# Seven products with eight sums: products that add up in shared PSUM banks, in the output projections and the feed-forward part of a hybrid block

## The chip, the cores and the metric

One Trainium2 chip, one of its cores. The metric is the device time of one execution in microseconds. PE is the matrix engine, DVE, ACT and POOL are the vector, scalar and GpSimd engines, SP issues most of the DMAs.

## The reference

A transformer block on one sequence of 1024 tokens of width 1024, in float32:

```python
h = rms_norm(x, norm1_gain)
hq, hf, hi, hg, sq, sk, sv, ga, gb = split_cols(h @ w_in, IN_SPLITS)
y_hg = (rms_norm(hgrn2_mixer(hq, hf, hi, lb)) * sigmoid(hg)) @ w_hg_out     # 1024 x 1024
y_sb = stick_breaking(rms_norm(sq), rms_norm(sk), sv) @ w_sb_out            # 1024 x 1024
x = x + (sigmoid(ga) * y_hg + sigmoid(gb) * y_sb) @ w_o                     # 1024 x 1024
gate, up = split_cols(rms_norm(x, norm2_gain) @ w_ffn_in, (2816, 2816))
x = x + (silu(gate) * up) @ w_ffn_out                                       # 2816 x 1024
```

The change concerns everything from `w_hg_out` on.

## The kernel before

Each float32 operand is split into a high part, a cast to float32r on ACT (`nc.scalar.copy`), and a low part, the rest by a subtraction on DVE or POOL (`tensor_sub`). `mm3` issues three matmuls for each block of 128 in the contracted dimension: high by high, high by low, low by high (lines L133, L134, L135). A tile of 128 x 512 of a product is one PSUM bank.

The five big products C = A B are computed by quarters: A, B and C are cut in two both ways, and seven products of sums of quarters replace eight. `A_TERMS` and `B_TERMS` say which quarters (11, 12, 21, 22) make up the operands of product m, `SUMS` to which quarters of C it is added, with a sign. There are ten operand sums (five for A, five for B) and twelve additions to C. `split` (L859 the sum, L861 the cast, L862 the low part) makes one operand; if a later product needs both quarters the sum goes to a scratch tile (`sum`, `as`, `bs`), otherwise over a quarter.

Three output projections (`w_hg_out`, `w_sb_out`, `w_o`) are objects of class `Product`, seven jobs each, 21 jobs of 48 matmuls. `job_steps(n)` runs job n tile by tile (four tiles of 12 matmuls) and, between the tiles, `prep` emits the operands of job n + 1: two pieces of the stationary operand, 128x1024 (`wh`, `wl`), and the moving operand in four rows of 128x512 (`u`). `load` fetches the quarters of job n + 2. `pd` has three banks, which the tiles use in turn; after each tile `done` (L934 ACT, first time; L936 DVE, later) adds the bank to one or two quarters of C. `finish_hg` and `finish_sb` gate with a sigmoid (`gated`, L961, L962) and mix (L969); `add_x1` (L974) adds to x. Which of the low parts go to DVE and which to POOL is written out by hand in the tables `LO_ON_VECTOR`, `LO_ON_POOL`, `GATE_..._ON_POOL`, `MIX_ON_POOL`.

`turn_h2` normalises and transposes the rows for the feed-forward part (L1053, L1057); sixteen such turns are woven into jobs 19 and 20 and into the first products after them. `b_op` (L1076 sum, L1078 cast, L1079 low part) makes the seven moving operands once. Then 22 tiles f of the hidden width run, each with seven products of 12 matmuls (`ffn_in`), in the order `ORDER`; the first two tiles are interleaved product by product. `a_tile` makes the stationary operands, two products in a block, with sums and low parts on POOL. Results go to quarter tiles `c` (L1194 ACT copies, L1196 DVE adds), then silu (L1199, L1200) and the product with the upper half (L1209, L1214); half of the activation is kept in SBUF (`acts`), half goes to DRAM (`d_act`) and comes back.

The last product (`ffn_out`, seven products of 132 matmuls in the order `SEQ`) makes both operands of each group of 128 rows in `o_tile`: the stationary one on DVE, the moving one on POOL. It uses four banks for each product, two sets in turn, and adds each bank to the one or two quarters of x that it belongs to (L1237).

PE's instructions stand in the order in which the code issues them; those of the other engines are put in order by the scheduler. All queues run in order. `block` keeps operands three blocks ahead (`wh` and `wl` have three buffers).

Of the kernel before, what the change touches and what calls it, by code (L numbers as in the profile page):

```python
# [34 lines left out]
def hybrid_block(ctx, tc, x, norm1_gain, w_in, lb_logits, hg_out_norm, sb_q_norm, sb_k_norm,  # L35
# [95 lines left out]
    def mm3(ps, lhs, rhs, start, stop):  # L131
        (lh, ll), (rh, rl) = lhs, rhs
        nc.tensor.matmul(ps, lh, rh, start=start, stop=False)  # L133
# [1 line left out]
        nc.tensor.matmul(ps, ll, rh, start=False, stop=stop)  # L135
# [716 lines left out]
    def split(e, terms, m, after, raw, scratch, hi, lo, e_lo=None):  # L852
        a, b, op = terms[m]
        src = raw(a)
        if b:
            later = {q for x in after for q in terms[x][:2]}
            free = [q for q in (a, b) if q not in later]
            dst = raw(free[0]) if free else scratch()
            e.tensor_tensor(dst, src, raw(b), op=op)  # L859
            src = dst  # L860
        nc.scalar.copy(hi, src)  # L861
        (e_lo or e).tensor_sub(lo, src, hi.bitcast(F32))  # L862

    LO_ON_VECTOR = {(0, 0), (0, 1), (1, 1), (2, 0), (3, 0), (4, 0), (5, 0), (6, 0), (7, 0), (8, 0), (8, 1), (9, 0), (16, 0)}
# [473 lines left out]
```

## Time and profile before

| | us |
|---|---|
| median of 3 runs | 2272.49 (2270.41 to 2273.56) |
| span of the profiled execution | 2272.3 |
| PE busy | 2099.6 (92%) |
| DVE busy | 1625.0 (72%) |
| POOL busy | 1147.2 (50%) |
| ACT busy | 1058.9 (47%) |

The profiled execution is shown by its span, from the first to the last instruction; its own time is not given apart from that, and the span lies 0.2 us under the median of the runs. A group's line gives busy time, then the mean duration in ns, then the idle time of the engine just before these instructions and what ended it. The line of one source or tile gives the shortest, median and longest duration in ns.

### The profile page before, as it was taken

How to read it: one execution, taken by the hardware profiler on the slowest of the kernel's cores; microseconds unless marked ns; L12 is line 12 of the kernel's file. 1: busy time of each engine (PE TensorE's matmuls, PEld its weight loads, DVE VectorE, ACT ScalarE, POOL GpSimd, SP SyncE). 2: the span in 40 equal slices, each digit the busy share in tenths (PEclk: the TensorE clock that was granted, in tenths of full speed). 3: DMA queues.
4: the chain of work that ended last, by engine and by line, in shares of the span. 5: the costliest groups of instructions: out<-in, count | busy, mean ns of one | idle time of the engine just before them, and what ended most of it. 6: DMA issues, size and time to landing. Idle time of an engine off the chain costs nothing. (4 is left out here: it accounts for less than half of the span.)

```text
span 2272.3 us, 29894 instructions
## 1 busy us (share of the span) xinstructions
PE 2099.6 (92%) x10981; PEld 1737.3 (76%) x10981; DVE 1625.0 (72%) x2205; ACT 1058.9 (47%) x1834; POOL 1147.2 (50%) x856
## 2 busy tenths in 40 slices
PE   7999999999999999899899887878899999998998
PEld 7888897978878778778777666656688888886685
DVE  5575758484678778877977999999844444457886
ACT  4353434442566666666655444336433333333342
POOL 4443434443222222313211546755688888889777
PEclk9999999999999999999999999988999999999999
DMA  4212121212222222222224153311112222253110
GB/s 148 75 47 75 41 63 56 64 56 87 78 82 54 69 74 67 72 67 70 66 67 169 50 185 105 132 56 56 56 57 72 67 70 89 70 210 114 39 50 37
DMA packets 181041, 179.69 MB, mean 79 GB/s; under 512 B 9064, under 2 KB 132384, under 8 KB 180896
## 3 DMA queue, kind: packets, MB, share of 16 engines
q1 hardware_dynamic: 179888, 176.09, 24.8%
q8 instruction: 86, 1.41, 0.3%
q10 hardware_dynamic: 1008, 1.70, 0.2%
q14 instruction: 59, 0.48, 0.1%
HBM read 125.86 MB, written 35.13 MB: 71 GB/s over the span
## 5 line engine op out<-in xcount | busy, mean ns | idle before, releaser
L133 PE MATMUL pd<-u,wh 128*128 128x512 f32 x952 | 390.9, 411 | 49.9 <-DVE u L936 20.3
L134 PE MATMUL pd<-u,wh 128*128 128x512 f32 x952 | 384.7, 404 | 18.6 <-DVE u L862 12.2
L135 PE MATMUL pd<-u,wl 128*128 128x512 f32 x952 | 384.6, 404 | 0.3 <-POOL wl L862 0.3
L133 PE MATMUL pd<-hT,wh 128*128 128x512 f32 (+1 forms) x920 | 378.7, 412 | 0.0
L134 PE MATMUL pd<-hT,wh 128*128 128x512 f32 (+1 forms) x920 | 359.8, 391 | 0.2 <-DVE hT L183 0.2
L135 PE MATMUL pd<-hT,wl 128*128 128x512 f32 (+1 forms) x920 | 359.6, 391 | 0.0
L116 POOL TENSOR_TENSOR wl<-wr,wh 128x1024 fp32r<-128x1024 f32 x72 | 188.0, 2613 | 338.7 <-ACT wh L115 305.4
L133 PEld LDWEIGHTS pd<-u,wh 128*128 128x128 f32 x952 | 184.7, 194 | 101.9 <-ACT u L934 21.8
L1196 DVE TENSOR_TENSOR c<-c,pd 128x512 f32<-128x512 f32 x160 | 106.4, 686 | 180.9 <-PE pd L135 97.3
L134 PEld LDWEIGHTS pd<-u,wh 128*128 128x128 f32 x952 | 184.9, 194 | 65.8 <-DVE u L862 14.5
L135 PEld LDWEIGHTS pd<-u,wl 128*128 128x128 f32 x952 | 184.1, 193 | 46.8 <-POOL wl L862 0.7
L862 POOL TENSOR_TENSOR wl<-u,wh 128x512 fp32r<-128x512 f32 (+1 forms) x99 | 169.6, 1723 | 96.3 <-ACT wh L861 80.8
L135 PEld LDWEIGHTS pd<-hT,wl 128*128 128x128 f32 x920 | 174.2, 189 | 39.3
L134 PEld LDWEIGHTS pd<-hT,wh 128*128 128x128 f32 x920 | 175.5, 191 | 23.5 <-DVE hT L183 0.4
L133 PEld LDWEIGHTS pd<-hT,wh 128*128 128x128 f32 x920 | 175.2, 190 | 23.4 <-ACT hT L182 0.2
L725 DVE TENSOR_TENSOR_SCAN kp<-kp,dsel 128x512 f32<-128x512 f32 (+3 forms) x128 | 131.8, 1030 | 44.5 <-ACT kp L718 44.4
L718 ACT ACTIVATE kp<-pz,rq 128x128 f32<-128x128 f32 (+2 forms) x192 | 112.5, 586 | 91.5 <-PE pz L714 80.7
L859 POOL TENSOR_TENSOR sum<-u,u 128x512 f32<-128x512 f32 (+1 forms) x67 | 120.7, 1804 | 62.4 <-DMA u<-in_w_hg_out 34.0
L133 PE MATMUL pd<-wh,hT 128*128 128x256 f32 x512 | 148.6, 290 | 0.0
L135 PE MATMUL pd<-wh,hT 128*128 128x256 f32 x512 | 145.1, 283 | 0.0
L134 PE MATMUL pd<-wl,hT 128*128 128x256 f32 x512 | 145.1, 283 | 0.0
L732 DVE TENSOR_TENSOR a<-a,kp 128x128 f32<-128x128 f32 (+2 forms) x192 | 130.2, 678 | 13.2
(247 smaller groups left out, 4869.3 us busy)
## 6 DMA issues: line engine op xcount, KB each, us to landing
wr<-in_w_in SPq DMA_DIRECT2D x72, 512.0 KB, 3.7
wr<-in_w_ffn_in SPq DMA_DIRECT2D x22, 512.0 KB, 4.5
u<-in_w_ffn_in SPq DMA_DIRECT2D x22, 512.0 KB, 5.3
u<-in_w_ffn_out SPq DMA_DIRECT2D x8, 1024.0 KB, 7.8
qh<-qh SPq DMA_DIRECT2D x48, 128.0 KB, 2.3
ql<-ql SPq DMA_DIRECT2D x48, 128.0 KB, 4.1
d_act<-c SPq DMA_DIRECT2D x20, 256.0 KB, 4.5
xt<-in_x SPq DMA_DIRECT2D x8, 512.0 KB, 8.6
```

The source lines that it names most:

```text
L116: nc.gpsimd.tensor_sub(lo, raw, hi.bitcast(F32))
L133: nc.tensor.matmul(ps, lh, rh, start=start, stop=False)
L134: nc.tensor.matmul(ps, lh, rl, start=False, stop=False)
L135: nc.tensor.matmul(ps, ll, rh, start=False, stop=stop)
L718: last["sig"] = [nc.scalar.activation(t[:, 0:w], ps[:, 0:w], AF.Sigmoid, scale=rq[:, n_, col:col + 1]) for n_, t in enumerate((kp, a))]
L725: nc.vector.tensor_tensor_scan(rev, rev, dsel[:, HS - w:][:, ::-1], initial=0.0, op0=ALU.mult, op1=ALU.max)
L732: nc.vector.tensor_mul(a[:, 0:w], a[:, 0:w], kp[:, 1:w + 1])
L859: e.tensor_tensor(dst, src, raw(b), op=op)
L862: (e_lo or e).tensor_sub(lo, src, hi.bitcast(F32))
L1196: nc.vector.tensor_tensor(C[c], C[c], M[m], op=ALU.add if sign > 0 else ALU.subtract)
```

## The change

The seven products are taken in another form, with eight operand sums, four for A and four for B, each of one quarter and an earlier sum, written in place over a quarter (`A_STEPS`, `B_STEPS`: target, two sources, operation). With P1 to P7 the products, C11 = P1 + P2, C12 = P1 + P6 + P5 + P3, C22 = P1 + P6 + P7 + P5, C21 = P1 + P6 + P7 + P4. Products 1, 6, 7, 4 are added up in the same PSUM banks (`CHAIN`), products 5 and 3 in another set, product 2 stands alone; after each product the running total is read once, into the one quarter `INTO[m]`. A product that doesn't open a group (`OPENS`) starts its matmuls without clearing the bank.

```diff
-    d_act = dp.tile([2, NF // 2, P, HS], F32, name="d_act")
+    d_act = dp.tile([3, NF // 2, P, HS], F32, name="d_act")
...
-    A_TERMS = {1: (11, 22, ALU.add), 2: (21, 22, ALU.add), 3: (11, None, None), 4: (22, None, None),
-               5: (11, 12, ALU.add), 6: (21, 11, ALU.subtract), 7: (12, 22, ALU.subtract)}
...
-    SUMS = {1: ((11, 1), (22, 1)), 2: ((21, 1), (22, -1)), 3: ((12, 1), (22, 1)), 4: ((21, 1), (11, 1)),
-            5: ((11, -1), (12, 1)), 6: ((22, 1),), 7: ((11, 1),)}
+    A_STEPS = {5: (21, 21, 22, ALU.add), 6: (21, 21, 11, ALU.subtract), 7: (11, 22, 21, ALU.subtract),
+               3: (12, 12, 21, ALU.subtract)}
+    A_SRC = {1: 11, 2: 12, 5: 21, 6: 21, 7: 11, 3: 12, 4: 22}
+    B_STEPS = {5: (11, 12, 11, ALU.subtract), 6: (11, 22, 11, ALU.subtract), 7: (12, 22, 12, ALU.subtract),
+               4: (21, 21, 11, ALU.subtract)}
+    B_SRC = {1: 11, 2: 21, 5: 11, 6: 11, 7: 12, 3: 22, 4: 21}
+    INTO = {1: 11, 2: 11, 5: 22, 6: 12, 7: 22, 3: 12, 4: 21}
+    OPENS, CHAIN = (1, 2, 5), (1, 6, 7, 4)
+    FIRST, FINAL = (1, 5, 6, 4), (2, 7, 3, 4)
...
+    def split(e, src, hi, lo):
         nc.scalar.copy(hi, src)
-        (e_lo or e).tensor_sub(lo, src, hi.bitcast(F32))
+        e.tensor_sub(lo, src, hi.bitcast(F32))
+
+    def chain_mm(ps, lhs, rhs, m, k, nk):
+        mm3(ps, lhs, rhs, m in OPENS and k == 0, k == nk - 1, m not in OPENS)
+
+    def four_banks(m):
+        if m in CHAIN:
+            return [dbank(), dbank(), dbank(), pbank("po", 1)]
+        return [pbank(t) for t in ("pt", "pt", "pz", "pz")]
...
             def stationary(c):
...
-                split(nc.gpsimd, A_TERMS, m, after, lambda q: self.raw("a", q)[:, :, c * 256:(c + 1) * 256],
...
-                      nc.vector if (7 * phases.index(self) + i, c) in LO_ON_VECTOR else None)
+                sum_step(self.a_sum, A_STEPS, m, raw)
+                split(nc.vector, raw(A_SRC[m]), hi, lo)
             def moving(c):
...
+                ks = slice(2 * c, 2 * c + 2)
+                raw = lambda q: self.raw("b", q)[:, ks, :]
+                sum_step(nc.vector, B_STEPS, m, raw)
+                split(nc.vector, raw(B_SRC[m]), *(u[:, ks, :] for u in sides[1]))
...
+            if m not in FIRST:
+                nc.vector.tensor_add(dst, dst, ps)
+            elif m not in FINAL:
+                nc.scalar.copy(dst, ps)
+            if m in FINAL:
+                finish(c, 4 * (c // 10 - 1) + j, c % 10 - 1, dst, ps if m in FIRST else dst)
...
-        Product((4, 2, 1, 7, 5, 3, 6), w_quarter(w_hg_out, lambda q: unit1, False),
-        Product((4, 5, 1, 7, 2, 3, 6), w_quarter(w_sb_out, lambda q: unit2 if q == 22 else unit1, False),
-        Product((3, 5, 4, 1, 7, 2, 6), lambda q: mixed[q // 10 + q % 10 * 10],
+    SEQ43, SEQ34 = (1, 2, 5, 6, 7, 4, 3), (1, 2, 5, 6, 7, 3, 4)
...
+    a_order = [(f, m) for f in range(3) for m in (1, 2)]
+    a_order += [(0, 5), (0, 6), (1, 5), (0, 7), (0, 3), (0, 4), (1, 6), (2, 5), (1, 7), (1, 3), (1, 4)]
+    for f in range(2, NF):
+        n = [(f + 1, m) for m in (1, 2)] if f + 1 < NF else []
+        a_order += [(2, 6)] if f == 2 else [(f, 5), (f, 6)]
+        a_order += n[:1] + [(f, 7)] + n[1:] + [(f, 3), (f, 4)]
...
+        both = wp.tile([P, 2, 4, P], F32R, tag=("wh", "wl")[n % 2], name="wh")
+        sum_step(nc.gpsimd, A_STEPS, m, raw)
+        split(nc.vector if m in (1, 2, 4) else nc.gpsimd, raw(A_SRC[m]), both[:, 0], both[:, 1])
...
             hi = wp.tile([P, 2, HS], F32R, tag="wh", name="wh")
             lo = wp.tile([P, 2, HS], F32R, tag="wl", name="wl")
-            for n, (e, terms, raw) in enumerate(((nc.vector, A_TERMS, acts), (nc.gpsimd, B_TERMS, w_out))):
-                split(e, terms, m, tuple(A_TERMS), lambda q: raw[q, g // 4][:, g % 4, :], lambda: scratch()[:, n],
+            sum_step(nc.vector, A_STEPS, m, A)
+            if m in (6, 4):
+                sum_step(nc.vector, B_STEPS, m, B)
+            split(nc.vector, A(A_SRC[m]), hi[:, 0], lo[:, 0])
+            split(nc.vector, B(B_SRC[m]), hi[:, 1], lo[:, 1])
+            if m in (1, 2):
+                sum_step(nc.gpsimd, B_STEPS, {1: 5, 2: 7}[m], B)
...
+    rest = {6: (7, nc.vector), 7: (3, nc.gpsimd), 9: (4, nc.vector)}
```

In the feed-forward tiles the products of tile f now run as 5, 6, then product 1 of the next tile, 7, product 2 of the next tile, 3, 4; the operands are made six products ahead (`a_ahead`), one product in a buffer. Eight turns of the first rows stand in job 20, the others among the first four products after it. The hand-written tables are gone; the gating and mixing are all on DVE. In the changed kernel the sum is L861, the cast L864, the low part L865; the reads of PSUM are L937, L939, L965, L977, L1157, L1159, L1169, L1171, L1228. Only one quarter of the activation stays in SBUF, three go through DRAM, and one of these as well as one quarter of `w_ffn_out` is loaded twice, because the sums overwrite them.

POOL's queue in the second output projection (`u` are quarters of the stationary operand, `sum` is scratch, `wl` low parts; 4x256 and 1024 are the same number of columns), before:

```order
L859 TENSOR_TENSOR sum<-u_12886,u_12888 128x1024 x2
L859 TENSOR_TENSOR u_12888<-u_12888,u_12779 128x4x256 x2
L862 TENSOR_TENSOR wl<-u_12779,wh 128x1024
L859 TENSOR_TENSOR sum<-u_12886,u_12779 128x1024 x2
L859 TENSOR_TENSOR u_12779<-u_13163,u_12779 128x4x256 x2
L859 TENSOR_TENSOR u_13163<-u_13163,u_12886 128x4x256 x2
L862 TENSOR_TENSOR wl<-sum,wh 128x1024
L862 TENSOR_TENSOR wl<-u_12888,wh 128x1024 x2
L862 TENSOR_TENSOR wl<-u_12779,wh 128x1024 x2
```

and after:

```order
L861 TENSOR_TENSOR u_12880<-u_12880,u_12882 128x4x256 x2
L861 TENSOR_TENSOR u_12880<-u_12880,u_12703 128x4x256
L861 TENSOR_TENSOR u_12703<-u_12882,u_12880 128x4x256
L861 TENSOR_TENSOR u_12791<-u_12791,u_12880 128x4x256
L861 TENSOR_TENSOR u_12880<-u_12880,u_12703 128x4x256
L861 TENSOR_TENSOR u_12703<-u_12882,u_12880 128x4x256
L861 TENSOR_TENSOR u_12791<-u_12791,u_12880 128x4x256
```

The low parts have left POOL's queue here; eight sums in place over the quarters are all that it has in this projection.

DVE's queue in the last product, in the product with the most sums, before (product 7, where the moving operand's sum and low part stand on POOL):

```order
L859 TENSOR_TENSOR sum<-u_18364,u_17881 128x512
L862 TENSOR_TENSOR wl<-sum,wh 128x512
L859 TENSOR_TENSOR sum<-u_18364,u_17881 128x512
L862 TENSOR_TENSOR wl<-sum,wh 128x512
L859 TENSOR_TENSOR sum<-u_18366,u_17883 128x512
L862 TENSOR_TENSOR wl<-sum,wh 128x512
```

and after (product 6):

```order
L861 TENSOR_TENSOR u_17262<-u_17262,u_14536 128x512
L861 TENSOR_TENSOR u_16393<-u_17256,u_16393 128x512
L865 TENSOR_TENSOR wl<-u_17264,wh 128x512
L865 TENSOR_TENSOR wl<-u_17232,wh 128x512
L861 TENSOR_TENSOR u_17262<-u_17262,u_14536 128x512
L861 TENSOR_TENSOR u_16393<-u_17256,u_16393 128x512
L861 TENSOR_TENSOR u_17264<-u_17264,u_15551 128x512
```

Both sums and both low parts of a group stand on DVE now, and POOL has none of this product.

More of the change, by code (lines that the diff above doesn't have):

```diff
@@ L852, in split @@
[L852 to L864, printed above, removed]
@@ L1159, in load_x1q, with silu, act_done, ffn_done @@
         nc.sync.dma_start(u, d_x1[4 * r:4 * r + 4, :, h * HS:(h + 1) * HS].rearrange("t p c -> p t c"))
+    D_ACT = (12, 21, 22)
+    banks, C = {}, {}
+    def silu(c):
+        s = pbank("pz")
+        order(nc.scalar.activation(s, c, AF.Sigmoid), last["rs"])
+        nc.vector.tensor_mul(c, c, s)
+    def act_done(f, half, a, b):
+        g, q = f // 2, 10 * (half + 1) + f % 2 + 1
+        if q == 11:
+            if g % 4 == 0:
+                acts[q, g // 4] = unit2(F32)
+            nc.vector.tensor_mul(acts[q, g // 4][:, g % 4, :], a, b)
+        else:
+            nc.vector.tensor_mul(a, a, b)
+            nc.sync.dma_start(d_act[D_ACT.index(q), g], a)
+    def ffn_done(f, m, ps):
+        c = INTO[m]
+        if m == 4:
+            act_done(f, 0, C.pop((f, 11)), ps)
+            return
+        if m in FIRST:
+            C[f, c] = tmp("c") if c == 11 else mp.tile([P, HS], F32, tag="m2", name="c")
+            nc.scalar.copy(C[f, c], ps)
+            return
+        nc.vector.tensor_add(C[f, c], C[f, c], ps)
+        if c < 20:
+            silu(C[f, c])
+        if m == 3:
+            act_done(f, 1, C.pop((f, 12)), C.pop((f, 22)))
+    def ffn_step(n, k):
+        f, m = a_order[n]
+        key = f, "p" if m in CHAIN else "t"
+        if k == 0:
+            a_ahead(n + 6)
+            if m in OPENS:
+                banks[key] = dbank() if m == 1 else pbank("po", 1) if m == 2 else pbank("pt")
+        ps, w = banks[key], a_ops[f, m]
+        bh, bl_ = bop[m]
+        chain_mm(ps, (w[:, 0, k, :], w[:, 1, k, :]), (bh[:, k, :], bl_[:, k, :]), m, k, 4)
+        if k == 3:
+            del a_ops[f, m]
+            ffn_done(f, m, ps)
+    def ffn_in(n):
+        return [(0.65, lambda k=k: ffn_step(n, k)) for k in range(4)]
     def o_tile(m, g):
@@ L1246, in step @@
+    def ffn_out(n):
+        m = SEQ34[n]
+        key = "p" if m in CHAIN else "t"
+        if m in OPENS:
+            banks[key] = four_banks(m)
+        ps = banks[key]
         def step(g, j):
@@ new lines, in hybrid_block @@
+    for n in range(6, len(a_order)):
+        if n in rest:
+            b_rest(*rest[n])
+        if a_order[n] == (16, 1):
+            load_w_out(11, 0, unit2)
+        run(ffn_in(n))
+    for i, u in ((1, unit1), (2, unit1)):
+        load_w_out(11, i, u)
+    load_x1q(11, unit1)
+    for i in range(3):
+        load_w_out(12, i, unit1)
+    for i in range(3):
+        load_act(12, i, unit1)
+    for i in range(3):
+        load_w_out(21, i, unit2)
+    for i in range(3):
+        load_w_out(22, i, unit1)
@@ L1293, in hybrid_block @@
+    for i in range(3):
+        load_act(21, i, unit2)
+    for n, m in enumerate(SEQ34):
+        if m == 2:
+            for i in range(3):
+                load_act(22, i, unit1)
+            load_x1q(22, unit2)
+        if m == 5:
+            load_x1q(12, unit2)
+        if m == 7:
             for i in range(3):
                 load_act(12, i, unit1)
-        if n == 4:
+            load_x1q(21, unit2)
+        if m == 3:
             for i in range(3):
-                load_w_out(21, i, unit2)
+                load_w_out(21, i, unit1)
```

323 lines of the change are left out of this document (103 added, 220 removed).

## Prediction

> **What bounds the kernel now.** I read the busy time by stage first, then the stage's groups by shape, then single instructions in order of time. The table of stretches (busy us and count for each engine, then the granted clock) is cut where the work changes: everything before the output projections; nineteen of their twenty-one product jobs; the last two jobs with the transposes of the second norm and the first two feed-forward tiles; the twenty other tiles; the last product.
>
> ```profile
> core 0: us, PE busy (x) PEld busy (x) DVE busy (x) ACT busy (x) POOL busy (x), PEclk, DMA share, GB/s
> 0.00:1246.20 1246.20, 1171.63 (x7138) 1009.53 (x7139) 890.94 (x1376) 650.69 (x1119) 399.35 (x387) 1.00 0.25 74
> 1246.20:1534.30 288.10, 232.91 (x913) 179.65 (x912) 274.70 (x285) 119.32 (x192) 169.00 (x67) 0.91 0.31 109
> 1534.30:1635.40 101.10, 81.65 (x329) 62.66 (x329) 90.80 (x115) 52.88 (x111) 62.69 (x40) 0.88 0.12 42
> 1635.40:2026.90 391.50, 391.50 (x1680) 315.12 (x1679) 184.76 (x249) 146.54 (x263) 313.94 (x237) 1.00 0.27 81
> 2026.90:2272.30 245.40, 221.89 (x927) 170.38 (x925) 183.84 (x182) 89.42 (x150) 202.19 (x128) 1.00 0.23 82
> ```
>
> Call the last four A, R, C and D. What PE needs at least comes from an undisturbed piece of its timeline:
>
> ```profile
> 1532.02 0.39 PE L135 MATMUL pd<-u,wl 128*128 128x512 f32 x1
> ...
> 1534.82 0.40 PE L135 MATMUL pd<-u,wl 128*128 128x512 f32 x1
> 1535.05 0.60 PE L1057 MATMUL pt<-ident,hn 128*128 128x128 f32 x4
> 1535.40 0.48 PE L133 MATMUL pd<-u,wh 128*128 128x512 f32 x1
> ```
>
> Twelve matmuls from start to start take 2.80 us, 0.233 each; four transposes delay the next matmul by about 0.35 us. So A needs 19 x 48 x 0.2333 = 212.8 us of its 288.1; R 264 matmuls and 64 transposes, 61.6 + 5.6 = 67.2 of 101.1; C 1680 matmuls, 392 of 391.5, so PE is the bound there; D 924 matmuls, 215.6 of 245.4, of which some 4 us are the drain after the last matmul. There are 75, 34 and 25 us to be had in A, R and D, and nothing in C.
>
> What fills those? In A, DVE is busy for 95%, but its instructions are stretched:
>
> ```profile
> L862 DVE TENSOR_TENSOR u<-u,u x54: 673/680/2897, 1247.7 to 1546.5; 128x512 fp32r<-128x512 f32 x54
> L936 DVE TENSOR_TENSOR u<-u,pd x64: 672/675/686, 1276.9 to 1461.1; 128x512 f32<-128x512 f32 x64
> L859 POOL TENSOR_TENSOR u<-u,u x18: 2409/2802/3399, 1252.8 to 1489.0; 128x1024 f32<-128x1024 f32 x18
> L859 POOL TENSOR_TENSOR wr<-wr x33: 1282/1296/1745, 1573.2 to 1987.3; 128x512 f32<-128x512 f32 x33
> ...
> 1265.58 1.21 DVE L862 TENSOR_TENSOR wl<-sum,wh 128x1024 fp32r<-128x1024 f32 x1
> 1266.87 2.79 POOL L859 TENSOR_TENSOR sum<-u,u 128x1024 f32<-128x1024 f32 x1 [2.97 <-DVE wl L862]
> ...
> 1365.65 11.66 POOL L859 TENSOR_TENSOR u<-u,u 128x1024 f32<-128x1024 f32 x4
> 1371.76 3.36 DVE L862 TENSOR_TENSOR wl<-sum,wh 128x1024 fp32r<-128x1024 f32 x1
> ```
>
> Minimum, median, maximum in ns: a DVE add of two SBUF tiles takes 0.68 us or up to 2.9; one with a PSUM input never over 0.69. The 128x1024 form takes 1.21 us while POOL is idle (at 1265.58), and 3.36 while POOL runs four sums back to back: 1.21 plus nearly one POOL instruction. So the two engines take turns on these operations, and what counts is the sum of both at their undisturbed durations. Stage A by shape:
>
> ```profile
> L862 POOL TENSOR_TENSOR wl<-u,wh 128x1024 fp32r<-128x1024 f32 x20 | 54.5, 2726 | 61.9 <-ACT wh L861 61.8
> L859 POOL TENSOR_TENSOR u<-u,u 128x1024 f32<-128x1024 f32 x18 | 50.5, 2823 | 0.5
> L859 POOL TENSOR_TENSOR sum<-u,u 128x1024 f32<-128x1024 f32 x11 | 29.7, 2712 | 21.0 <-DVE wl L862 16.2 <-DMA u<-in_w_sb_out 3.1 <-DVE u L969 1.4
> L862 POOL TENSOR_TENSOR wl<-sum,wh 128x1024 fp32r<-128x1024 f32 x7 | 18.8, 2691 | 22.4 <-ACT wh L861 22.4
> L969 POOL TENSOR_TENSOR u<-u,u 128x512 f32<-128x512 f32 x8 | 13.7, 1720 | 8.1 <-DVE u L962 8.0
> ...
> L862 DVE TENSOR_TENSOR u<-u,u 128x512 fp32r<-128x512 f32 x51 | 51.1, 1037 | 3.4 <-POOL wl L862 3.4
> L862 DVE TENSOR_TENSOR u<-sum,u 128x512 fp32r<-128x512 f32 x24 | 37.7, 1588 | 0.0
> L859 DVE TENSOR_TENSOR sum<-u,u 128x512 f32<-128x512 f32 x23 | 37.3, 1641 | 2.0 <-DMA u<-in_w_o 1.8
> L962 DVE TENSOR_TENSOR u<-u,m 128x512 f32<-128x512 f32 x30 | 36.6, 1222 | 1.2 <-ACT m L961 0.8
> L859 DVE TENSOR_TENSOR u<-u,u 128x512 f32<-128x512 f32 x32 | 31.7, 1023 | 2.1 <-DMA u<-d_osb 2.1
> L974 DVE TENSOR_TENSOR u<-u,pd 128x512 f32<-128x512 f32 x34 | 21.6, 678 | 2.8 <-PE pd L135 2.8
> L862 DVE TENSOR_TENSOR wl<-sum,wh 128x1024 fp32r<-128x1024 f32 x5 | 10.4, 2085 | 0.0
> L862 DVE TENSOR_TENSOR wl<-u,wh 128x1024 fp32r<-128x1024 f32 x6 | 9.9, 1643 | 0.7 <-ACT wh L861 0.7
> L969 DVE TENSOR_TENSOR u<-u,u 128x512 f32<-128x512 f32 x8 | 7.6, 952 | 0.1
> ```
>
> POOL 56 x 2.41 + 8 x 1.28 = 145; DVE 168 x 0.68 + 11 x 1.21 = 128; together 273 of 288.1 us. That is the bound of A. The 98 PSUM reads (L936, L974; 66 us) hid inside POOL's turns. D is the same:
>
> ```profile
> L862 DVE TENSOR_TENSOR wl<-sum,wh 128x512 fp32r<-128x512 f32 x55 | 71.5, 1301 | 3.2 <-ACT wh L861 2.9
> L859 DVE TENSOR_TENSOR sum<-u,u 128x512 f32<-128x512 f32 x55 | 57.8, 1058 | 33.4 <-POOL wl L862 32.2
> L862 DVE TENSOR_TENSOR wl<-u,wh 128x512 fp32r<-128x512 f32 x21 | 28.1, 1344 | 17.8 <-ACT wh L861 17.8
> ...
> L862 POOL TENSOR_TENSOR wl<-sum,wh 128x512 fp32r<-128x512 f32 x54 | 87.2, 1618 | 4.5 <-ACT wh L861 4.5
> L859 POOL TENSOR_TENSOR sum<-u,u 128x512 f32<-128x512 f32 x52 | 84.8, 1630 | 6.8 <-DVE wl L862 2.8 <-POOL wl L862 0.7
> L862 POOL TENSOR_TENSOR wl<-u,wh 128x512 fp32r<-128x512 f32 x22 | 33.4, 1523 | 26.0 <-ACT wh L861 16.1 <-DVE sum L859 5.7 <-PE pt L133 1.9
> ```
>
> DVE 131 x 0.68 = 89, POOL 128 x 1.28 = 164: 253 against 245.4 us.
>
> **A rule weighed.** The Trainium skill, page "SBUF — State Buffer", section "SBUF: two separate sides", says that VectorE (an operation with two SBUF inputs) and GpSimd share a port pair as an exclusive lock, held for the whole instruction, so that the other blocks. The 3.36 us row agrees. Had they only shared bandwidth, the mean durations would travel with the instructions: that is the first rival, and its 2310 us stands against the 2172 that the lock gives.
>
> **The change, part by part.** PE's matmuls are the same in number and kind (PSUM accumulation across products adds none), so nothing comes or goes there.
>
> Stage A. All low halves move to DVE, and POOL keeps sums of the stationary operand only. Nineteen operands are made in this stage, each with four DVE subtractions of 128x1024 (two stationary, two moving): 76; moving sums for eleven products, two each: 22; so 98 x 1.21 = 118.6. Gating and mixing from SBUF, 12 + 12 + 16: 40 x 0.68 = 27.2. POOL keeps 24 sums, 24 x 2.41 = 57.8. Turns together: 203.6 us, below PE's 212.8. DVE also reads PSUM 52 times (16 + 16 + 20) at 0.676, 35 us; if all of it hides in POOL's turns the bound is PE, 212.8; if none, DVE with POOL is 238.8. Before, all of it hid, but POOL had 145 us to hide it in, now 58 for 35. Halfway is 221, plus 2% for queues in order (before, 5% above its bound): 225. Gain 63. ACT casts as many elements as before, at 41% busy (119.32 of 288.1), so it stays cover.
>
> Evacuation. 84 reads of PSUM in the three products (24 by ACT, 60 by DVE) replace 144 of three rotating banks (32 and 112), since products 6, 7, 4 and 3 add up in the bank; a bank is written again four tiles, 4 x 2.8 us, after its last write, not three. PE's waits for the readers (L936, and L934 on ACT) go; what is late next is DVE's operand work, priced above. Where product 7 now waits in PE's queue for a read of product 6, everything behind it on PE waits too, which is why the read's place in DVE's and ACT's order matters.
>
> Stage R. The change makes seventeen products ahead of the steady part, not fourteen: for equal work before is 101.1 + 3 x 2.8 = 109.5. PE needs 300 x 0.2333 + 5.6 = 75.6.
>
> ```profile
> L1053 DVE SCALAR_TENSOR_TENSOR hn<-u,rs,u x16: 737/752/2994, 1530.4 to 1582.3; 128x512 f32<-128x512 f32 x16
> ```
>
> DVE: six 1.21 for the last operand, 16 hn at 0.75, 24 + 16 operations on the moving operands, ten low halves and two products at 0.68: 54.7, and some 3 us of small ones. POOL: ten sums, ten low halves, four of operand 3, 24 x 1.28 = 30.7. Turns 88.4, with 22 PSUM reads (15 us) at most 103. The eight turns of the first rows now stand in one job, not two, so 95. Gain 14.5.
>
> Stage C. Per tile POOL falls from 12 operations (15.4 us) to 8 (10.2), DVE's share of the turns rises from 1.4 to 2.7: 13 of 19.6 us. PE hides it all. The new handover is that product 7 adds to the bank of product 6 one product (2.8 us) later, and ACT must have copied that bank by then. Such copies before:
>
> ```profile
> L1194 ACT ACTIVATE c<-pd 128x512 f32<-128x512 f32 x80 | 45.3, 591 | 35.4 <-PE pd L135 34.6 <-POOL wl L862 0.9
> ```
>
> 0.59 us each, and held up by POOL for 0.9 us in all, so it fits. Cost 0; if each of 20 tiles waits 1 us, 20. SP's queue gets 11 more stores and 9 more loads: three quarters of the activation go through DRAM, not two, and one activation and one weight quarter are loaded twice, some 11 MB more. C moved 81 GB/s with PE full, so the stores are hidden. 1644 x 0.2333 = 383.5 us.
>
> Stage D. DVE now makes both operands: 154 low halves and 66 sums, 220 x 0.68 = 150; POOL only 22 sums, 28. Turns 178, with 28 PSUM adds 197: under PE's 215.6. The product with two sums has four DVE operations per group, 2.72 against 2.8 us, the tightest place. With 4 us of drain and 3 for handovers 223. Gain 22. Three loads of the activation's last quarter are issued only when product 1 frees their slots, and stand in DVE's order ahead of product 2's later groups; no row shows such a late load, so 0 to three groups of 2.8 us, 8; I take 0, since D moved only 82 GB/s on average, and leave 8 to the range.
>
> Sum: 1246.2 + 225 + 95 + 383.5 + 223 = 2172.7; the profiled span of 2272.3 is the median of the runs, 2272.49, within 0.2 us, so about 2172.
>
> **The rivals.** (1) Slower: the stretched durations belong to DVE and not to POOL's turns. Then A's 98 cost 1.85 each and the 40 cost 1.20: 264 with the PSUM reads, over its 95% share 277; R's DVE time at the same ratio, (57.7 x 1.6 + 15) over its 90%, 120; D 220 x 1.20 + 19 = 283. 1246.2 + 277 + 120 + 383.5 + 283 = 2310. For it: the means. Against: minimum and median at 0.68, and L936. It decides once a two-input DVE operation in D stays above 1.03 us ((245.4 - 19) / 220). 4%.
> (2) Turns not hidden: PSUM reads and POOL's sums add up in A (239), R comes to 108, D to 231 because of the tight product and the reloads: 2208. For it: DVE would be at full load in A. 20%.
> (3) PE is the bound everywhere: 214, 82, 383.5, 220: 2146. For it: prepared operands are a job ahead. Against: in-order queues, and R's 88 us of turns. 12%.
> (4) ACT's copy of product 6 stands behind casts that wait for POOL's sums in every tile: at five us a tile the gain is gone, 2272, and beyond that it is slower. Against: the 0.9 us of L1194, and POOL gets lighter. 3%.
> The forecast, 2155 to 2195, has 61%.
>
> **How the numbers follow.** Range 2140 to 2225: rivals 2 and 3 with some room; left out are 1, 4 and worse mixes. About 0.2% is what a measurement of this kernel tells from no change. Faster 0.93, same 0.02, slower 0.05.
>
> **What would show it.** After, in A a two-input DVE 128x1024 has a median near 1.21 and POOL some 60 us; A ends by about 1471, with the clock back above 0.95; C keeps 0.233 us per matmul; in D no PE wait on POOL's low halves is left. Wrong if DVE stays at 95% in A and D with long means (rival 1), if C's rate falls (rival 4), or if PE waits in D for reloaded quarters.

## The result, and the profile after

The changed kernel takes 2188.77 us (median of 4 runs, 2185.45 to 2189.44), the kernel before 2271.45 (2269.07 to 2273.56) on the same chip: ratio 0.9633, 95% interval 0.9619 to 0.9647, so 83 us less. The profiled execution has a span of 2186.7 us and took 2188.52.

The table of stretches of the changed kernel, cut at the same matmuls as the prediction's stages (after 912, 1212 and 2856 matmuls, counted from the first of the output projections); columns as in the prediction:

```profile
core 0: us, PE busy (x) PEld busy (x) DVE busy (x) ACT busy (x) POOL busy (x), PEclk, DMA share, GB/s
1245.70:1483.80 238.10, 221.20 (x914) 175.64 (x913) 217.29 (x190) 113.16 (x148) 75.11 (x26) 0.96 0.38 127
1483.80:1583.25 99.45, 83.00 (x366) 65.86 (x365) 78.39 (x126) 56.73 (x118) 46.58 (x30) 0.91 0.32 98
1583.25:1968.20 384.95, 384.27 (x1645) 308.93 (x1644) 135.13 (x199) 139.06 (x235) 198.22 (x149) 1.00 0.27 86
1968.20:2186.70 218.50, 211.44 (x925) 172.71 (x923) 166.30 (x246) 84.38 (x148) 30.84 (x20) 1.00 0.32 113
```

| stage | before, same matmuls | predicted | after | gain |
|---|---|---|---|---|
| ahead | 1246.2 | 1246.2 | 1245.7 | 0.5 |
| A | 288.1 | 225 | 238.1 | 50.0 |
| R | 109.5 | 95 | 99.5 | 10.0 |
| C | 383.5 | 383.5 | 385.0 | -1.5 |
| D | 245.0 | 223 | 218.5 | 26.5 |

So the span is 14.0 us over the predicted 2172.7, made of +13.1 in A, +4.5 in R, +1.5 in C, -4.5 in D and -0.5 ahead.

DVE's and POOL's operations in A of the changed kernel, minimum, median and maximum in ns (first the low halves and moving sums, then an evacuation, then POOL's sums):

```profile
L865 DVE TENSOR_TENSOR u<-u,u x40: 1211/1219/3485, 1248.2 to 1477.3; 128x1024 fp32r<-128x1024 f32 x40
L861 DVE TENSOR_TENSOR u<-u,u x22: 1211/1223/3419, 1256.2 to 1471.8; 128x1024 f32<-128x1024 f32 x22
L937 DVE TENSOR_TENSOR u<-u,pz x8: 673/675/685, 1271.6 to 1419.9; 128x512 f32<-128x512 f32 x8
L861 POOL TENSOR_TENSOR u<-u,u x24: 2411/3224/3404, 1249.4 to 1454.2; 128x1024 f32<-128x1024 f32 x24
```

The medians of DVE are now the undisturbed 1.22 us, but single ones still last 3.4: nearly one POOL sum (2.41) more. Reads of PSUM are untouched (0.69 at most), as before. PE's waits in A and in R, from the waits of each stretch (releaser, us in total, times, longest):

```profile
PE pz L133 <- DVE u L937: 8.9, 3, 5.1
PE pz L133 <- DVE u L977: 5.0, 2, 3.5
PE pd L134 <- DVE u L865: 2.4, 1, 2.4
PE pt L133 <- DVE u L977: 0.7, 1, 0.7
...
PE pd L134 <- DVE u L865: 10.2, 2, 9.8
PE pt L1058 <- DVE hn L1054: 3.8, 2, 3.4
PE pt L134 <- DVE u L865: 2.4, 1, 2.4
```

A lost 17.0 us in waits, 14.6 of them (the reads, L937 and L977) where product 5 opens the four banks that product 2 used just before it. The timeline of DVE, POOL and PE at the longest of them:

```profile
1272.23 2.84 DVE L861 TENSOR_TENSOR u<-u,u 128x1024 f32<-128x1024 f32 x1
1274.99 2.88 DVE L965 TENSOR_TENSOR u<-m,u 128x512 f32<-128x512 f32 x1
1277.79 3.36 DVE L861 TENSOR_TENSOR u<-u,u 128x1024 f32<-128x1024 f32 x1
1281.07 0.68 DVE L937 TENSOR_TENSOR u<-u,pz 128x512 f32<-128x512 f32 x1
...
1271.18 8.88 POOL L861 TENSOR_TENSOR u<-u,u 128x1024 f32<-128x1024 f32 x3 [2.36 <-DVE wl L865]
...
1276.29 0.39 PE L135 MATMUL pz<-u,wl 128*128 128x512 f32 x1
1281.80 0.80 PE L133 MATMUL pz<-u,wh 128*128 128x512 f32 x1 [5.12 <-DVE u L937]
1282.39 0.63 PE L134 MATMUL pz<-u,wh 128*128 128x512 f32 x1
...
1286.66 0.63 PE L135 MATMUL pz<-u,wl 128*128 128x512 f32 x1
1287.09 0.54 PE L133 MATMUL pd<-u,wh 128*128 128x512 f32 x1
```

Three POOL sums in a row stretch three DVE operations (two sums of 128x1024 and a gating multiplication) to 9.1 us together, and the read that PE waits for (1281.07) stands behind them in DVE's order. The wait has a tail: from 1281.80 to 1287.09 twelve matmuls start some 0.43 us apart, not 0.233, and the granted clock from 1282.4 to 1287.1 is 0.50. Over A these tails are some 8 us; 17 + 8 is nearly the whole of A's excess of 25.3 us over PE's 212.8.

### The profile page after: what moved, and what is told of

Same layout as the page of the kernel before. It is cut to its first block, busy times and chain, and to the rows that moved or that the text cites. A ratio compares the mean times of both kernels' runs of the same rounds, so it can differ in the third digit from the quotient of the medians.

```text
span 2186.7 us, 29330 instructions
## 1 busy us (share of the span) xinstructions
PE 2072.3 (95%) x10981; PEld 1733.8 (79%) x10981; DVE 1480.4 (68%) x2128; ACT 1041.3 (48%) x1762; POOL 749.3 (34%) x611
## 5 line engine op out<-in xcount | busy, mean ns | idle before, releaser
L864 ACT CAST wh<-u 128x512 fp32r<-128x512 f32 (+1 forms) x280 | 183.8, 684 | 232.9 <-PE po L135 88.4
L134 PE MATMUL pd<-u,wh 128*128 128x512 f32 x496 | 198.1, 399 | 12.6 <-DVE u L865 12.6
L865 DVE TENSOR_TENSOR wl<-u,wh 128x512 fp32r<-128x512 f32 (+1 forms) x196 | 169.3, 900 | 55.7 <-ACT wh L864 50.7
L133 PE MATMUL pd<-u,wh 128*128 128x512 f32 x496 | 198.0, 399 | 0.7 <-ACT c L1169 0.7
L861 POOL TENSOR_TENSOR u<-u,u 128x1024 f32<-128x1024 f32 (+1 forms) x46 | 105.1, 2303 | 198.6 <-DVE u L972 55.1
L135 PE MATMUL pd<-u,wh 128*128 128x512 f32 x352 | 139.5, 396 | 0.0
L134 PEld LDWEIGHTS pd<-u,wh 128*128 128x128 f32 x496 | 94.3, 190 | 36.2 <-DVE u L865 13.9
L718 ACT ACTIVATE a<-pz,rq 128x128 f32<-128x128 f32 (+2 forms) x192 | 112.2, 585 | 2.7 <-PE pt L758 2.7
L758 PE MATMUL pt<-ident,a 128*128 128x128 f32 x576 | 89.9, 277 | 24.9 <-DVE a L732 14.9
```

The source lines that it names most:

```text
L133: nc.tensor.matmul(ps, lh, rh, start=start, stop=False, skip_group_check=adds)
L134: nc.tensor.matmul(ps, lh, rl, start=False, stop=False, skip_group_check=adds)
L135: nc.tensor.matmul(ps, ll, rh, start=False, stop=stop, skip_group_check=adds)
L718: last["sig"] = [nc.scalar.activation(t[:, 0:w], ps[:, 0:w], AF.Sigmoid, scale=rq[:, n_, col:col + 1]) for n_, t in enumerate((kp, a))]
L758: nc.tensor.transpose(tp[:, s * P:(s + 1) * P], a[:, b * P:(b + 1) * P], ident)
L861: e.tensor_tensor(raw(to), raw(a), raw(b), op=op)
```

## The experiments

Two explanations for the missing 13 us of A stood against each other: the work of DVE and POOL together (capacity), or a single badly placed read (handover). Behind them stood the question whether the turns are the cause of the gain at all. Each run was timed beside the kernel before, and its ratio to it carries a 95% interval. The lengths of stages are those of the one profiled execution of each kernel, cut at the same matmuls.

**1. Low halves of the stationary operands back on POOL** (in `stationary`):

```
-                split(nc.vector, raw(A_SRC[m]), hi, lo)
+                split(nc.gpsimd, raw(A_SRC[m]), hi, lo)
```

> The changed kernel with the low halves of the stationary operands of the three output products back on POOL, nothing else. Theory 1 (turns): what limits stage A is the sum of DVE's operations on two SBUF inputs and of POOL's, since they take turns. 38 low halves in A go from 1.21 us (DVE) to 2.41 us (POOL), so the turns grow from 203.6 to 249 us; at the share that before had (273 of 288) A takes about 262 us where it took 238, and with R the time is 2210 to 2225 us. Rival 2 (banks): the gain came from fewer reads of PSUM and from products that add up in a bank. Those are untouched, so 2184 to 2194. Rival 3 (DVE's load alone): DVE gets 46 us of work less in A, so A falls and the time is 2170 to 2182.

Measured 2224.14 us, ratio 0.9780 (0.9765 to 0.9794); A 271.3, R 101.7. Inside the range of the turns, above their 262 for A. The new products and banks are all there, and two thirds of A's gain is gone: rivals 2 and 3 fall as accounts of the whole gain. What the new products are worth by themselves comes in experiment 9.

**2. The kernel before, all low halves on DVE**:

```
-                      nc.vector if (7 * phases.index(self) + i, c) in LO_ON_VECTOR else None)
+                      nc.vector)
...
-                      hi[:, n], lo[:, n])
+                      hi[:, n], lo[:, n], nc.vector)
```

> The kernel before, with its own products, sums and banks, but all low halves of the operands of the output projections and of the last product made on DVE. Theory 1 (turns): in A 27 low halves of 128x1024 go from 2.41 to 1.21 us, turns 273 to 240, A about 253 us instead of 288; in D 76 of 128x512 go from 1.28 to 0.68, turns 253 to 207, D about 225 instead of 245; R gains some 5. Together 2205 to 2225 us from 2271, so more than half of the whole gain without the new products. Rival 2 (banks and fewer PSUM reads): 2265 to 2275. Rival 3 (the long means belong to DVE): DVE is at 95% of A already, so more work on it makes A longer: over 2280.

Measured 2232.01 us, ratio 0.9814 (0.9797 to 0.9832): 41 us of gain, half of the change's, without any of its new sums, but 7 us above the expected range. A 265.2 (expected 253), R 100.3, D 226.2 (225), and C 390.1, 6.6 us more than in the kernel before; one wait of 3.9 us for a copy on ACT is part of that, the rest is open. So moving low halves alone pays as the turns say, with A's part too large in the estimate: 29 sums and 10 gating and mixing operations stayed on POOL, with one low half (104 us busy together).

**3. Stationary sums on DVE too**:

```
-                accumulate(m1, lambda: unit2, finish_hg), nc.gpsimd),
+                accumulate(m1, lambda: unit2, finish_hg), nc.vector),
```

and the same for the two other products.

> The changed kernel with the stationary sums of the three output products on DVE too, so that POOL has nothing to do in stage A. 24 sums of 128x1024 cost 1.21 us instead of 2.41. Theory 1a (capacity): A at 238.1 us is the sum of the turns and the unhidden PSUM reads, 203.6 + 35.2 = 238.8; the new sum is 122 x 1.21 + 27.2 + 35.2 = 210 us, below PE's 212.8, so A takes 220 to 230 and the time is 2173 to 2182. Theory 1b (a late read at one handover): A lost 25 us because product 5 opens the banks of product 2 while DVE is behind; DVE's row no longer has 2.8 us operations in it, so the read comes sooner, and the result is much the same, 2170 to 2182, with the idle time before product 5 mostly gone. Rival: DVE as one full queue in order is what makes the read late, whatever POOL does; DVE's own work rises from 181 to 210 us, so 2189 to 2200.

Measured 2165.69 us, ratio 0.9522 (0.9506 to 0.9538). Stage A and its operations:

```profile
1247.10:1459.90 212.80, 212.80 (x914) 171.18 (x913) 196.66 (x212) 113.81 (x148) 4.30 (x2) 1.00 0.43 142
...
L865 DVE TENSOR_TENSOR wl<-u,wh x38: 1212/1219/1727, 1248.1 to 1459.2; 128x1024 fp32r<-128x1024 f32 x38
```

A is PE's bound to the tenth, 212.8 us, better than expected: DVE got 24 sums more and was busy for 20.6 us less (217.29 to 196.66). Undisturbed, the sums it took over are 24 x 1.13 = 27 us (1.13 is the distance between starts, below), so without them DVE's own work was some 169.5 us, and in the changed kernel it was stretched by 48 us for 24 x 2.41 = 58 us of POOL. The rival (a full DVE queue is late whatever POOL does) falls.

**4. Products 2 and 1 in the other order**, so that product 1 stands between products 2 and 5:

```
+    TWO43, TWO34 = (2, 1, 5, 6, 7, 4, 3), (2, 1, 5, 6, 7, 3, 4)
+    FIRST_P, FINAL_P = (2, 5, 6, 4), (1, 7, 3, 4)
```

used by the three output products, their evacuations, and with the third product's stationary quarters taken when they are needed.

> The changed kernel with products 1 and 2 of each output product in the other order (2, 1, 5, 6, 7, ...), so that product 1 stands between product 2 and product 5, which take the same four banks. The amount of work on every engine is the same. Theory 1b (a late read at one handover): the idle times of 1.5 to 5.1 us before product 5's first matmuls, some 17 us with the slower matmuls behind them 25, go; A takes 215 to 225 us and the time is 2167 to 2178. Theory 1a (capacity): A is DVE's and POOL's 238.8 us of work, PE only waits at another place; 2184 to 2194.

Measured 2192.13 us, ratio 0.9638 (0.9623 to 0.9652): the same as the changed kernel. A 240.9. PE's waits in A:

```profile
PE pd L134 <- DVE u L865: 12.9, 2, 6.5
PE pd L135 <- DVE wl L865: 5.0, 1, 5.0
PE pd L133 <- ACT wh L864: 1.1, 1, 1.1
```

The waits for banks are gone, and 19 us of waits for operands stand in their place. So the handover was only where the shortage showed; my theory 1b falls, 1a stays.

**5. Low halves of the moving operand of the last product back on POOL**:

```
-            split(nc.vector, B(B_SRC[m]), hi[:, 1], lo[:, 1])
+            split(nc.gpsimd, B(B_SRC[m]), hi[:, 1], lo[:, 1])
```

> The changed kernel with the low halves of the moving operand of the last product back on POOL, nothing else. Theory 1 (turns): 77 low halves in D go from 0.68 to 1.28 us, the turns grow from 178 to 224 us, over PE's 215.6, and 28 PSUM adds of 0.68 us hide behind them in part: D takes 226 to 240 us where it took 218.5, and the time is 2196 to 2211 us. Rival 2 (banks and fewer PSUM reads made D shorter): those stay, 2185 to 2192 us.

Measured 2211.24 us, ratio 0.9721 (0.9700 to 0.9742); D 241.2 where it was 218.5, a us above the expected range; all other stages within 0.4 us. This one line takes back 22.7 of D's 26.5 us.

**6. Work on POOL that nobody wants**, on the base of experiment 3:

```
+                if m in A_STEPS:
+                    nc.gpsimd.tensor_sub(wp.tile([P, 4, 256], F32, tag="wr", bufs=2, name="unused"), raw(A_SRC[m]), hi.bitcast(F32))
```

> The changed kernel with all sums of the output products on DVE (2165.7 us, A 212.8 us), and with 24 subtractions of 128x1024 added on POOL, whose results nobody reads: the low half of each operand that has a sum, once more. Theory 1 (turns): DVE has to wait for an engine whose result nobody wants. Turns in A are 175 + 58 = 233 us, with PSUM reads at most 268: A takes 235 to 260 us, DVE's two-input operations are stretched to 2 us and more, and the time is 2188 to 2212 us. Rival (order): A gained in the kernel without POOL since nothing on DVE and PE waits for POOL's sums any more; here nothing waits for them either, so 2163 to 2170 us.

Measured 2215.93 us, ratio 0.9741 (0.9723 to 0.9758): 50 us more than its base and 4 above the expected range; A 254.2. More than the turns is in this: ACT waited 10.1 us for POOL to read the stationary high half, whose buffer it had to write again. Experiment 11 leaves that out.

**7. Everything after the attention on DVE**: experiment 3, and

```
-        sum_step(nc.gpsimd, A_STEPS, m, raw)
-        split(nc.vector if m in (1, 2, 4) else nc.gpsimd, raw(A_SRC[m]), both[:, 0], both[:, 1])
+        sum_step(nc.vector, A_STEPS, m, raw)
+        split(nc.vector, raw(A_SRC[m]), both[:, 0], both[:, 1])
...
-                sum_step(nc.gpsimd, B_STEPS, {1: 5, 2: 7}[m], B)
+                sum_step(nc.vector, B_STEPS, {1: 5, 2: 7}[m], B)
...
-    rest = {6: (7, nc.vector), 7: (3, nc.gpsimd), 9: (4, nc.vector)}
+    rest = {6: (7, nc.vector), 7: (3, nc.vector), 9: (4, nc.vector)}
```

> The changed kernel with all sums and all low halves, of the output products, the feed-forward and the last product, on DVE: POOL has nothing to do after the attention. Theory 1 (turns): R lasts as long as DVE's queue, which is full from its start to the end of the 10 to 13 us stall before product 6; 24 operations of 1.28 us (POOL) become 24 of 0.68 us, so R takes 84 to 92 us instead of 100. C has 8 more operations per tile on DVE, 5.4 of 19.6 us, beside 6.9 that are there, and stays at 385. D stays at 218, where PE is the bound. 2151 to 2160 us. Rival: in C the operands' chains now stand in DVE's queue ahead of the reads of PSUM, and PE waits for banks: over 2168 us.

Measured 2145.92 us, ratio 0.9435 (0.9416 to 0.9453), better than the range. The stages:

```profile
1246.80:1459.60 212.80, 212.80 (x914) 171.18 (x913) 196.41 (x213) 114.32 (x149) 0.00 (x0) 1.00 0.42 143
1459.60:1545.40 85.80, 80.14 (x366) 63.93 (x365) 83.09 (x159) 56.32 (x117) 0.00 (x0) 0.96 0.37 114
1545.40:1930.30 384.90, 384.23 (x1645) 308.91 (x1644) 233.98 (x348) 136.93 (x235) 0.00 (x0) 1.00 0.28 86
1930.30:2144.30 214.00, 210.15 (x925) 173.09 (x923) 164.61 (x266) 84.36 (x148) 0.00 (x0) 1.00 0.32 115
```

R falls from 99.5 to 85.8 (in experiment 3 it was 100.5, with one wait of 13.3 us before product 6). C is as long with 149 operations more on DVE. D falls to 214.0, which I had not expected: POOL's 20 sums there (30.8 us busy) still cost 4.5 us.

**8. Product 5 of the second tile ahead of product 6 of the first**, on the base of 7:

```
-    a_order += [(0, 5), (0, 6), (1, 5), (0, 7),
+    a_order += [(0, 5), (1, 5), (0, 6), (0, 7),
```

> As the kernel with everything on DVE, and product 5 of the second feed-forward tile comes ahead of product 6 of the first, so that PE has one more product (2.8 us) to do while DVE still makes operand 6. Theory: R's stall before product 6 is a late operand at the end of a full DVE queue; one product more before it takes 2 to 3 us off the stall and off the time, 2149 to 2157 us. Rival: DVE's queue sets the end of the next products (7, 3, 4) too, and the 2.8 us come back there: same time as without.

Measured 2150.10 us, ratio 0.9450 (0.9431 to 0.9470). No gain: experiment 7 has no wait before product 6 left to shorten (0.3 us), and here R takes 88.3 with a wait of 2.5. The premise, a stall that outlasts the move to DVE, was wrong; the time lies in the expected range only because everything on DVE came out faster than forecast. 3.3 us more stand ahead of A, in code that is the same; in the profiled executions of all the kernels with that code this part lasts 1245.2 to 1250.1 us, so differences of this size between single executions say nothing.

**9. The kernel before, all of it on DVE**: both operands of the output projections and of the last product, and gating and mixing (`nc.gpsimd` to `nc.vector` in `stationary`, `gated`, `finish_sb`, `o_tile`).

> The kernel before, with its own products, sums and banks, and with all sums, low halves, gating and mixing of the output projections and both operands of the last product on DVE; the first feed-forward operands stay on POOL. It separates the form of the products from the place of the work. DVE in A then has 176 two-input operations of 128x512, 67 of 128x1024 and 66 reads of PSUM. Reckoned by the rows' durations (0.68, 1.21, 0.68) that is 246 us; reckoned by the distance between starts that the kernel without POOL in A shows (0.60, 1.13, 0.60) it is 221 us, still over PE's 212.8. Theory 1 with the distances: A 222 to 240 us, R some 90, C 390, D at PE's bound with 219 to 223: 2170 to 2190 us, so the place alone gives as much as the whole change. Theory 1 with the rows' durations: A 246 or more, 2193 to 2215 us. Rival (the new form is what lets DVE keep up): DVE with 144 reads and 112 more small operations falls behind in order, A stays at 265 as with the low halves alone, over 2215 us.

Measured 2202.47 us, ratio 0.9690 (0.9666 to 0.9714). Stage A:

```profile
1248.30:1492.00 243.70, 224.84 (x914) 173.68 (x913) 236.98 (x342) 121.62 (x193) 0.00 (x0) 0.97 0.38 130
```

The two kinds of PSUM reads in it, from 1246 to 1490:

```profile
L936 DVE TENSOR_TENSOR u<-u,pd 128x512 f32<-128x512 f32 x64 | 42.7, 680 | 3.4 <-PE pd L135 2.8
...
L974 DVE TENSOR_TENSOR u<-u,pd 128x512 f32<-128x512 f32 x34 | 22.0, 679 | 1.7 <-PE pd L135 1.7
```

The expectation counted 66 reads of PSUM in A; there are 98, and 66 us is the time that they take. With 98, the sum of the rows' durations is 267 us, longer than A itself, and the sum of the distances between starts 240; DVE was busy for 237.0 of A's 243.7. So the distances give DVE's time, and that 246 came near A, and the time into the range of the durations, was luck. DVE is busy for 97% with no POOL at all. The place of the work alone is worth 70.5 us (2272.98 for the kernel before beside this run), nearly the 83 of the change; new form and all of the work on DVE together (experiment 7) are worth 129. This is what the new form is worth in A: with the same placement, its fewer PSUM reads and sums, and moving operands made in pieces twice as large, bring A from 243.7 to PE's 212.8 (experiment 3), 31 us. D is 214.9, nearly what experiment 7 has.

**10. The weights' low halves ahead of this stage on DVE as well** (`load_w`), on the base of 7:

```
-        nc.gpsimd.tensor_sub(lo, raw, hi.bitcast(F32))
+        nc.vector.tensor_sub(lo, raw, hi.bitcast(F32))
```

> The kernel with everything after the attention on DVE (2145.9 us), and the 72 low halves of the weights ahead of it, 128x1024, on DVE instead of POOL as well. It asks whether the rule carries to a stage where PE is at 94% and waits for DVE's other operations. Theory 1 (turns): 188 us of POOL (2.62 each) become 82 of DVE; DVE's operations there (887 us of 1247) lose their stretching, PE's 75 us of idle time shrink by 5 to 25 us, 2120 to 2141 us. Rival: in this stage DVE is the engine that PE waits for (its scans and PSUM reads in chains), POOL's turns matter little, and 82 us more in DVE's queue delay it: 2146 to 2190 us.

Measured 2138.45 us, ratio 0.9403 (0.9383 to 0.9423), the shortest of all versions; its interval touches that of experiment 7, so the step from 7 to 10 (7.5 us between medians, on two chips) is likely, not settled. An operation of the attention, in 7 and in 10:

```profile
L732 DVE TENSOR_TENSOR a<-a,kp 128x384 f32<-128x384 f32 x80 | 60.2, 752 | 7.2
```

```profile
L732 DVE TENSOR_TENSOR a<-a,kp 128x384 f32<-128x384 f32 x80 | 46.7, 584 | 5.4
```

DVE's operations do lose their stretching there: DVE has some 82 us of work more (72 x 1.13) and is busy for only 25 us longer (886.9 and 912.2). But PE's wait for this operation went only from 15.0 to 14.6 us, and the part ahead of A from 1246.8 to 1242.6, 2.6 us under the shortest of the others. So little of what the turns cost DVE there reaches PE; what sets the end of that stage was not looked for.

**11. Unwanted work on POOL, without the buffer**, on the base of 3 (in `moving`, for the products that have a stationary sum):

```
+                if m in A_STEPS:
+                    hi = sides[1][0][:, ks, :].bitcast(F32)
+                    unused = wp.tile([P, 2, HS], F32, tag="wr", bufs=2, name="unused")
+                    nc.gpsimd.tensor_sub(unused, hi, hi)
```

> The experiment with unused subtractions on POOL once more, without its side effect: there ACT waited 10.1 us for POOL to have read a buffer before it could write it again. Here the 24 subtractions of 128x1024 read the high half of a moving operand, whose buffer is written again only several jobs later, so that nothing waits for them but by the turns. Base: all sums of the output products on DVE, A 212.8 us, 2165.7 us. Theory 1 (turns): A grows to 228 to 252 us, DVE's operations are stretched again, 2180 to 2206 us. Rival (the growth of 41 us came through the buffers): A stays within 212 to 218, 2163 to 2172 us.

Measured 2193.26 us, ratio 0.9654 (0.9637 to 0.9671). A, and the operations in it:

```profile
1248.90:1484.10 235.20, 220.79 (x913) 172.86 (x913) 224.23 (x208) 110.34 (x143) 105.69 (x26) 0.98 0.39 131
...
L865 DVE TENSOR_TENSOR u<-u,u x38: 1210/1220/2920, 1251.4 to 1482.9; 128x1024 fp32r<-128x1024 f32 x38
L941 DVE TENSOR_TENSOR u<-u,pz x8: 677/682/684, 1271.1 to 1424.6; 128x512 f32<-128x512 f32 x8
```

A grows by 22.4 us, nearly the 25.3 that POOL's 24 wanted sums cost the changed kernel, and no engine waits in this trace for one of these subtractions. That is the turns by themselves. R grew too, by 7.3 us; its first weights load into the buffer that the unwanted results used, so only A is read here.

**12. Copies instead of subtractions**: the last line of 11 becomes twice `nc.gpsimd.tensor_copy(unused, hi)`.

> The same place and base, with 48 copies of 128x1024 on POOL (one input each, f32 to f32) instead of the 24 subtractions. It asks whether any work on POOL makes DVE wait, or only operations with two SBUF inputs there. Theory 1 as the prediction had it speaks of two-input operations on both sides; the rows of before show none of POOL's copies beside DVE's sums. If one-input work on POOL waits and is waited for as well, A grows with POOL's time: 48 copies at an estimated 1.3 us, twice the 0.7 us that a 128x512 TENSOR_SCALAR takes on POOL, 62 us in all, A 228 to 255 us, 2180 to 2210 us. If not, A stays at 212.8 to 216 and the time at 2163 to 2170 us. I expect the first, with 6 in 10.

Measured 2187.95 us, ratio 0.9629 (0.9613 to 0.9645); A 228.5, 15.7 more than the base, at the lower end of the first case. Operations with one SBUF input on POOL hold DVE up as well:

```profile
L916 POOL COPY unused<-u x24: 1041/1976/23138, 1260.2 to 1470.0; 128x1024 f32<-128x1024 f32 x24
...
L865 DVE TENSOR_TENSOR u<-u,u x38: 1211/1226/2065, 1248.9 to 1473.1; 128x1024 fp32r<-128x1024 f32 x38
```

## Why the prediction was right, and where it was not

**The bound.** Shown: DVE's two-input operations and POOL's take turns, and that lengthens A and D. POOL work put back (1, 5) or put in for nothing (11) lengthens the stage; POOL work taken out (2, 3, 7) shortens it. Rival (1), the stretched durations belong to DVE, is out: its test was a mean above 1.03 us in D, and there are 0.78 and 0.69 there now:

```profile
L865 DVE TENSOR_TENSOR wl<-u,wh 128x512 fp32r<-128x512 f32 x150 | 110.3, 780 | 39.0 <-ACT wh L864 38.8
L861 DVE TENSOR_TENSOR u<-u,u 128x512 f32<-128x512 f32 x66 | 42.4, 686 | 5.4 <-DMA u<-d_act 5.3
```

**A: 225 predicted, 238.1 measured.** The step that failed is "halfway": half of the 35 us of PSUM reads were to hide in POOL's turns. Experiment 3 gives the account: 48 of POOL's 58 us lay on DVE's path. The sum with nothing hidden, 238.8, and rival (2)'s 239 lie next to the measured 238.1, but in part by luck: they add durations, and DVE's rows overlap; by distances DVE's own 169.5 and POOL's 57.8 make 227, and DVE was busy for 217.3 us of A and idle for 20.8, more than half of that waiting for casts on ACT. So A is not a full DVE queue from end to end. Late DVE operations, behind POOL's sums, stop PE at single places, and each such wait costs more than itself: some 8 of the 25.3 us are slow tails, a term that the prediction did not have. The sums are bounds and no price: turns alone and turns with all reads were 249 and 284 us in experiment 1 (measured 271.3), 240 and 306 in experiment 2 (265.2), 233 and 268 in experiment 11 (235.2). Why more hid in the kernel before is not shown.

**Evacuation.** Right that waits for readers shrink: in A of the kernel before they were 40.3 us, of the three rows here, after 14.6.

```profile
PE pd L133 <- DVE u L936: 20.3, 8, 5.8
PE pd L133 <- ACT u L934: 19.6, 5, 8.7
...
PE pd L133 <- DVE u L974: 0.4, 1, 0.4
```

That they go was wrong, and experiment 4 shows that taking them away gains nothing while POOL's sums still hold DVE up.

**R: 95 predicted, 99.5 measured.** What was mis-sized is the stage's place between 88 (all reads of PSUM hidden) and 103 (none). DVE is busy for 65.4 of R's first 71.2 us, and operand 6's low halves come late:

```profile
1483.80:1555.00 71.20, 54.75 (x249) 43.22 (x248) 65.35 (x109) 46.16 (x100) 30.02 (x18) 0.89 0.26 89
```

The PE row that waits for them, and DVE's:

```profile
1553.89 0.80 PE L134 MATMUL pd<-u,wh 128*128 128x512 f32 x1 [9.81 <-DVE u L865]
...
1549.23 1.73 DVE L865 TENSOR_TENSOR u<-u,u 128x512 fp32r<-128x512 f32 x1 [1.16 <-POOL u L865]
```

Without POOL it takes 85.8 (7), so the turns were the cause. One product more ahead of operand 6 bought nothing (8).

**C: 383.5 predicted, 385.0 measured.** Right. The new handover, product 7 on product 6's bank, costs one wait of 0.7 us in all 20 tiles:

```profile
PE pd L133 <- ACT c L1169: 0.7, 1, 0.7
```

So rival (4) is out, and the extra transfers stayed hidden at 86 GB/s.

**D: 223 predicted, 218.5 measured.** The mechanism was right, and one term was too large. PE's bound was reckoned with 0.2333 us per matmul; in D, where the bank changes every three matmuls, seven products of 132 take 29.9 to 30.2 us each in experiment 7, 0.227 per matmul: 210 us, not 215.6. The 3 us for handovers stand against 3.5 us of waits, but other ones: 0.7 us for a bank and 2.8 for DVE's low halves, in products 1 and 2, beside which POOL makes its sums. Product 6, with two sums the tightest place by the prediction, took 29.9 us, with no wait. Without POOL (7) no wait is left, and D is PE's 210 and the drain of some 4, 214.0. The late reload, bounded at 0 to 8 us, cost nothing: no wait of PE in D is for a DMA, and experiment 7 has the same reloads and no wait.

**The signs.** Medians near 1.21, C's rate, the clock above 0.95 in A (0.96) and no wait for POOL's low halves in D (POOL makes none there now) came as written. A's end by 1471 did not (1483.8), nor POOL's 60 us (75: its 24 sums took 71.7, as they wait for DVE too).

**The rule of the Trainium skill** that the prediction weighed ("SBUF — State Buffer", section "SBUF: two separate sides") agrees with the stretched rows: a DVE operation of 1.21 us that is held up lasts up to 3.4 us beside POOL's sums of 2.41. Which of the two goes first doesn't follow from the starts that a trace shows (experiment 11's 21.86 us row, below). Its clause that only POOL operations that read SBUF count against DVE's two-input ones is borne out as far as experiment 12 goes: a copy reads it, and counts. No run here had POOL work that does not read SBUF.

## What to carry to other kernels

Where DVE's two-input operations and POOL share a stage, add both engines' undisturbed times, once without and once with DVE's PSUM reads, and compare both sums with PE: in the changed kernel the turns alone (203.6 us) were below PE's 212.8, and A still took 238.1. An operation that POOL does in 2.41 us and DVE in 1.21 is no relief on POOL, even if nothing waits for it (experiment 11: 22 us for 24 of them). A wait that the profile names may only be the place where a shortage shows: before reordering around it, ask what holds up the engine behind it (experiment 4: 17 us of waits went, and 19 stood elsewhere). And count what a wait of PE does to the matmuls after it.

## What the runs showed of the hardware that I had not expected

- The turns are not even. In experiment 11 a subtraction on POOL began at 1276.16 and ended 21.9 us later, and until 1296 DVE ran on undisturbed, its 128x1024 operations 1.13 us apart; only then did POOL come in, and DVE wait:

```profile
1276.16 21.86 POOL L916 TENSOR_TENSOR unused<-u 128x1024 f32<-128x1024 f32 x1 [7.89 <-ACT u L864]
...
1293.92 1.22 DVE L865 TENSOR_TENSOR u<-u,u 128x1024 fp32r<-128x1024 f32 x1
1295.05 1.22 DVE L861 TENSOR_TENSOR u<-u,u 128x1024 f32<-128x1024 f32 x1
1296.25 2.85 DVE L865 TENSOR_TENSOR u<-u,u 128x1024 fp32r<-128x1024 f32 x1
1299.03 2.91 DVE L865 TENSOR_TENSOR wl<-u,wh 128x1024 fp32r<-128x1024 f32 x1
```

  The longest such subtraction lasted 24.0 us, the longest copy in experiment 12 23.1. POOL's operations in a row let DVE in after each one (three for three at 1271 to 1281 in the changed kernel). So in these stretches DVE's operations back to back passed POOL's, and POOL's did not pass DVE's. Why POOL came in at 1296 is not shown.
- After a wait of 5.1 us, PE ran at 0.43 us per matmul for 5.3 us; after 9.8 us, for 3.2 us; after waits of 0.8 to 1.5 us alone, not at all. The Trainium skill, "TensorE: Matmul & The Clock Gate", section "Part 1: The HAM clock gate (the "warmup" mystery)", has this as half the clock after an idle window of some 3.4 us, until a busy window has passed; the rows agree with the half clock (0.50 granted from 1282.4 to 1287.1). But waits of 3.0 and 2.4 us with 3.3 us of work between them (1366.99 and 1372.65 in the changed kernel) were followed by slow matmuls too, though neither is as long as that window.
- DVE's next operation starts before the row of the one before ends: 1.13 us apart at a duration of 1.22, 0.60 at 0.68. So sums of DVE's work go by the distances: in experiment 9 they give 240 us for 237.0 of busy time, the durations 267. The prediction and most of the expectations added durations.
